# Weight splits and modulation sums behind evictions in the planner's order

## The chip, the cores and the metric

The kernel runs on one core of one Trainium2 chip. The time is device microseconds of one execution, as the median of several runs. Besides that there is one profiled execution, from which every duration below is read.

## What is computed

One token sequence (256 tokens, 1024 channels) passes through two networks in a row, all in float32. Cut to what matters:

```python
# first block (one layer)
h = rms_norm(x, g_mix_pre);  proj = h @ w_in                 # 1024 x 5376: q, k, v, pool, u, v, gates
merged = sum of three gated branches (stick-breaking attention, multiscale pool, spatial gating)
x = x + rms_norm(merged @ w_out, g_mix_post)
x = x + rms_norm(square(relu(rms_norm(x, g_ff_pre) @ w_ff_in)) @ w_ff_out, g_ff_post)
# second block, layer i = 0 (convolution), 1 (attention)
mod = silu(c) @ ada_w[i] + ada_b[i]                          # 1024 x 6144: sh1, sc1, g1, sh2, sc2, g2
h = rms_norm(x, mix_norm_g[i]) * (1 + sc1) + sh1
x = x + g1 * mixer(h)                                        # conformer_conv or moba_attention
h = rms_norm(x, mlp_norm_g[i]) * (1 + sc2) + sh2
x = x + g2 * (square(relu(h @ mlp_w1[i])) @ mlp_w2[i])
```

## The kernel before

All weights are streamed once from HBM, in one list called `stream`. An element of the list is 1 MB: either a `Half` (half of a weight block, 128 partitions x 2048 numbers) or an `Ada` (a quarter of one segment of the modulation weights). `issue_raw` (line 327) starts the load of the next elements into three `raw` buffers, by DMAs on the queue of SyncE (SP). `prep_one` (line 342) turns a landed element into what the engines use.

A `Half` is split into two float32r parts, since a float32 matmul is done as three float32r products: wH is the rounded copy (ScalarE, line 354) and wL the rest, raw minus wH (VectorE, line 355). Each is done in two parts of 128 x 1024, so a `Half` costs two ScalarE and two VectorE instructions. Four halves (two blocks) of wH and wL are held at a time (`W_SLOTS`). An `Ada` is not multiplied on TensorE at first: VectorE adds two products with the silu of c to an accumulator (line 383, two instructions of 128 x 1024). With the first quarter of a segment a bias row is loaded (line 377), and with some groups a GpSimd memset (line 370) and two gain rows (line 372). When a group is complete, `ada_finish` sums the accumulator over partitions by matmuls (line 395) and stores the rows, which `ada_load` brings back later.

`done` (line 431) is called when a block has been used: it frees its halves and calls `pump` (line 418), which prepares as many further elements as there are free slots. `need` does the same before a block is used. So the splits are traced, that is, written down by the program, between the work of one block and that of the next. Elements are prepared in two other places by `prep_one(by_part=True)`, for the first weights only.

What reads the results of TensorE are evictions: activations also are split into a high and a low part (`KM.split`, lines 508 and 509), the output of the stick-breaking attention is split by lines 820 and 821, gates are evicted by 851 and 852. The norms run over two token tiles: line 538 or 536 adds the parts of the sum, GpSimd raises it to the power -1/2 (line 539), VectorE scales, and TensorE transposes the result (line 514). `two_by_two` (line 893) is the stage with four jobs (two token tiles by two column blocks) and a norm after each token tile. `ff` (line 945) is the feed-forward, eight blocks in and eight blocks out. In the attention, line 1236 evicts the scores, lines 1238 to 1244 make the softmax and line 1253 transposes it.

The order of the instructions on each engine is not the order of tracing. A planner runs the traced program on a clock of its own: when an engine is free, it takes the instruction with the lowest number among those whose inputs are ready at that moment. The number is a counter, `tc.cur_priority`, that goes up by one with each traced instruction. On the chip each engine then works through its queue in exactly that order, whatever has become ready. In some stretches the order is the traced one by decree (`tc.manual_schedule`): all engines at the very start, and TensorE in the convolution stage.

Of the kernel before, what the change touches and what calls it, by code (L numbers as in the profile page):

```python
# [34 lines left out]
G0, G1 = (0, 1, 2, 3), (4, 5, 6, 7)  # L35
SB_AT = {(0, 0): (("s", G0),), (2, 1): (("c", G0),), (4, 1): (("o", G0), ("s", G1)), (6, 1): (("c", G1),), (8, 1): (("o", G1),)}
HOLD = 1
BASE_PAD = {"q4": 128, "hidH": 32, "ok": 144}
PUSH = {'pre': (0, 1, 0, 0, 0, 0), 'mix': (1, 2, 1, 2, 2, 1), 'ff': (1, 1, 1, 1, 1, 1, 1, 1, 1, 0, 1, 1, 1, 1, 1, 1), 'conv': (1, 4, 1), 'mlp': (1, 1, 1, 0, 1, 1, 1, 1, 1, 1, 1, 0, 1, 1, 0, 1), 'at': (0, 0, 0, 0)}

# [66 lines left out]
def net_kernel(ctx: ExitStack, tc: tile.TileContext, I, out):  # L107
# [8 lines left out]
    def nm(s):  # L116
        cnt[0] += 1
        return f"{s}_{cnt[0]}"
# [3 lines left out]
    def T(shape, tag, bufs, dt=F32):  # L122
        if tag in BASE_PAD and tag not in based:
            based.add(tag)
            sb.tile([P, BASE_PAD[tag]], F32, tag="pad" + tag, bufs=1, name=nm("pad"))
        return sb.tile(shape, dt, tag=tag, bufs=bufs, name=nm(tag))
# [7 lines left out]
    def dram(ap, offset, dims):  # L134
        return bass.AP(tensor=ap.tensor, offset=ap.offset + offset, ap=dims)
# [8 lines left out]
    stream = []  # L144
# [179 lines left out]
    st = {"raw": 0, "prep": 0, "gen": 0, "live": []}  # L324
# [15 lines left out]
    ada_ready = []  # L340

    def prep_one(by_part=False):
        i = st["prep"]
        it = stream[i]
        v = raws.pop(i)
        if isinstance(it, Half):
            kc, n = it.shape
            h = T([P, kc, n], "wH", W_SLOTS, F32R)
            l = T([P, kc, n], "wL", W_SLOTS, F32R)
            it.H, it.L = h, l  # L350
            st["live"].append(it)

            def part(p, q):
                act(h[:, p:q, :], v[:, p:q, :], AF.Copy)  # L354
                nc.vector.tensor_sub(l[:, p:q, :], v[:, p:q, :], h[:, p:q, :].bitcast(F32))  # L355

            m = kc // 2
            if by_part:
                st["prep"] += 1
                return [lambda: part(0, m), lambda: part(m, kc)]  # L360
            for p, q in ((0, m), (m, kc)):
                part(p, q)
        else:
            first = it.slot == 0 if len(it.group) == 1 else it.seg == it.group[0]
            if first and it.quarter == 0:
                acc_cur[0] = T([P, 2, D], "acc", 1)
                acc_cur[1] = T([P, 512], "adarow", 1)
                if 1 in it.group or 4 in it.group:
                    seg = 1 if 1 in it.group else 4
                    nc.gpsimd.memset(acc_cur[1], 1.0)  # L370
                    for n in range(2):
                        nc.sync.dma_start(acc_cur[1][32 * n:32 * n + 1, :],
                                          dram(I["mix_norm_g_2" if seg == 1 else "mlp_norm_g_2"],
                                               it.layer * D + n * 512, [[512, 1], [1, 512]]))
            acc = acc_cur[0][:, it.slot, :]
            if it.quarter == 0:
                nc.sync.dma_start(ada_init[0:1, :], dram(I["ada_b_2"], it.layer * 6 * D + it.seg * D, [[D, 1], [1, D]]))
                src = ada_init
            else:
                src = acc  # L380
            for c in range(2):
                k = it.quarter * 2 + c
                stt(acc, v[:, c, :], cond[:, k:k + 1], src, op0=ALU.mult, op1=ALU.add)  # L383
                src = acc
            if it.quarter == 3 and it.seg == it.group[-1]:
                ada_ready.append((it, acc_cur[0], acc_cur[1], st["gen"]))
        st["prep"] += 1
# [30 lines left out]
    def pump(limit=99):  # L418
        issue_raw()
        while st["prep"] < st["raw"] and limit > 0:  # L420
            it = stream[st["prep"]]
            if isinstance(it, Half):
                if len(st["live"]) >= W_SLOTS:
                    break
            elif ada_ready:
                break
            prep_one()
            issue_raw()
            limit -= 1

    def done(*blocks, limit=99):
        for b in blocks:
            for h in b.halves:
                st["live"].remove(h)
        ada_finish()
        st["gen"] += 1
        pump(limit)
# [154 lines left out]
    with tc.manual_schedule(engines={nc.tensor.engine, nc.vector.engine, nc.scalar.engine}):  # L592
# [17 lines left out]
        rst.append(norm_stats([x[1][:, half(n)] for n in range(2)]))  # L610
        hk.from_token_half(0, 0, h0[0])
        parts = prep_one(by_part=True)
        parts[0]()
        hk.from_token_half(0, 1, h0[1])
# [7 lines left out]
        v_part(1, 0)  # L622
        v_part(1, 1)
        parts = prep_one(by_part=True)
        for i in range(2):
            parts[i]()
# [646 lines left out]
    def flush(keep=0):  # L1273
        while len(pend) > keep:
            qk_trans(*pend.pop(0))

    for n in range(2):
        bq, bk = B["aq", n], B["ak", n]
        need(bq, bk)
        for t in range(NT):  # L1280
            for i, b in enumerate((bq, bk)):
                a = ts_job(hk, t, b)
                qn = qk_norm(a)
                if t == 1:
                    done(b)
                flush(HOLD)
                pend.append((n, t, i, qn))
# [85 lines left out]
```

## Time and profile before

| | |
|---|---|
| median of 3 runs | 994.72 us (992.79 to 997.69) |
| profiled execution, whole | 991.49 us |
| its span, first to last instruction | 989.8 us |
| busy TensorE, weight loads of it | 962.0 us, 790.5 us |
| busy VectorE, ScalarE, GpSimd | 709.7, 544.8, 63.4 us |
| wL subtractions (line 355) | 306, 1.22 us each |
| wH copies (line 354) | 306, 1.05 us each |
| modulation sums (line 383) | 84 and 12, 1.28 us each |
| read from HBM | 221.44 MB, 225 GB/s over the span |

In the timelines a row is the start in us from the span's start, the duration, the engine, the line, the operation, output and inputs by the program's names, the shapes, and how many like instructions follow each other in it. A bracket is the idle time of the engine before it and what ended it. PE is TensorE, DVE is VectorE, ACT ScalarE, POOL GpSimd, SP SyncE.

### The profile page before, as it was taken

What the parts mean: (1) busy time and instruction counts of PE and PEld (TensorE: products, weight loads), DVE (VectorE), ACT (ScalarE), POOL (GpSimd) and SP (SyncE); (2) the same over time, 40 slices, a digit from 0 to 9 for tenths busy, and PEclk for the clock granted to TensorE, in tenths of its full rate; (3) what the DMA queues carried; (4) which work ended last, traced back from release to release, by engine and by line L of the source; (5) the groups of instructions that cost most, each with busy time, mean ns of one, the idle gap of its engine ahead of it and who ended that gap; (6) DMA issues with size and microseconds to landing.
All of it is one profiled execution on the core that took longest, in us unless ns stands there. A gap on an engine that the chain in (4) does not pass through costs nothing.

```text
span 989.8 us, 12826 instructions
## 1 busy us (share of the span) xinstructions
PE 962.0 (97%) x4969; PEld 790.5 (80%) x4969; DVE 709.7 (72%) x914; ACT 544.8 (55%) x835; POOL 63.4 (6%) x88
## 2 busy tenths in 40 slices
PE   7999999999999999998999999999989999999998
PEld 5988879878788887864878888887867778888886
DVE  6758877788677777888678677768678486665553
ACT  5646765456655565423555665555576456555561
POOL 4102110010000000100000000001330000000000
PEclk9999999999999999999999999999999999999999
DMA  7788676578678986785258888875524246676531
GB/s 253 246 297 278 225 280 209 196 253 287 210 270 294 313 309 206 242 302 192 76 173 299 287 286 284 309 255 197 189 86 170 86 165 218 218 249 246 200 130 43
DMA packets 89731, 223.37 MB, mean 226 GB/s; under 512 B 4304, under 2 KB 8298, under 8 KB 89670
## 3 DMA queue, kind: packets, MB, share of 16 engines
q1 hardware_dynamic: 89670, 222.55, 65.0%
q8 instruction: 39, 0.64, 0.3%
q14 instruction: 22, 0.18, 0.0%
HBM read 221.44 MB, written 1.10 MB: 225 GB/s over the span
## 4 chain that ended last, share of the span: by engine, by line
PE 74%; DVE 13%; issue 4%; ACT 3%; DMA 3%; POOL 2%; POOLq 0%; SPq 0%; DVEq 0%; ACTq 0%
PE B L469 14%; PE A L456 13%; PE A L454 13%; PE A L455 13%; PE B L470 7%; DVE wL L355 5%; PE A L469 3%; DMA raw<-in_w_in_dram 2%; DVE acc L383 2%; ACT wH L354 2%; POOL rst L539 1%; PE A L461 1%; PE A L463 1%; PE A L462 1%; PE A L470 1%
## 5 line engine op out<-in xcount | busy, mean ns | idle before, releaser
L355 DVE TENSOR_TENSOR wL<-raw,wH 128x1024 fp32r<-128x1024 f32 x306 | 362.0, 1221 | 109.8 <-ACT wH L354 109.4
L354 ACT ACTIVATE wH<-raw 128x1024 fp32r<-128x1024 f32 x306 | 306.9, 1051 | 176.4 <-PE A L456 99.4
L469 PE MATMUL B<-hHL,wH 128*128 128x512 f32 x576 | 204.1, 399 | 0.0
L470 PE MATMUL B<-hHL,wL 128*128 128x256 f32 x576 | 162.0, 281 | 0.0
L454 PE MATMUL A<-wH,hidH 128*128 128x512 f32 x384 | 151.2, 394 | 0.0
L456 PE MATMUL A<-wH,hidL 128*128 128x512 f32 x384 | 150.0, 391 | 0.0
L455 PE MATMUL A<-wL,hidH 128*128 128x512 f32 x384 | 149.8, 390 | 0.0
L454 PE MATMUL A<-wH,hHL 128*128 128x512 f32 (+1 forms) x336 | 130.9, 390 | 1.5 <-ACT wH L354 0.8
L469 PEld LDWEIGHTS B<-hHL,wH 128*128 128x128 f32 x576 | 108.3, 188 | 27.4 <-ACT wH L354 0.8
L455 PE MATMUL A<-wL,hHL 128*128 128x512 f32 (+1 forms) x336 | 129.5, 385 | 0.5 <-DVE wL L355 0.5
L456 PE MATMUL A<-wH,hHL 128*128 128x512 f32 (+1 forms) x336 | 129.5, 386 | 0.0
L383 DVE SCALAR_TENSOR_TENSOR acc<-raw,cond,acc 128x1024 f32<-128x1024 f32 x84 | 107.9, 1285 | 17.2 <-DMA raw<-in_ada_w_dram 16.7
L470 PEld LDWEIGHTS B<-hHL,wL 128*128 128x128 f32 x576 | 109.0, 189 | 0.7
L454 PEld LDWEIGHTS A<-wH,hidH 128*128 128x128 f32 x384 | 72.1, 188 | 18.0 <-issue 3.3
L456 PEld LDWEIGHTS A<-wH,hidL 128*128 128x128 f32 x384 | 72.1, 188 | 15.5
L455 PEld LDWEIGHTS A<-wL,hidH 128*128 128x128 f32 x384 | 72.2, 188 | 14.3
L454 PEld LDWEIGHTS A<-wH,hHL 128*128 128x128 f32 x336 | 63.7, 190 | 15.0 <-issue 1.6
L455 PEld LDWEIGHTS A<-wL,hHL 128*128 128x128 f32 x336 | 63.7, 190 | 12.9 <-DVE wL L355 1.0
L456 PEld LDWEIGHTS A<-wH,hHL 128*128 128x128 f32 x336 | 63.8, 190 | 12.6 <-issue 0.3
L469 PE MATMUL A<-hHL,wH 128*128 128x512 f32 x192 | 68.2, 400 | 2.1 <-DVE hidL L821 2.1
L470 PE MATMUL A<-hHL,wL 128*128 128x256 f32 x192 | 53.7, 280 | 0.0
L976 ACT ACTIVATE rs<-B 128x256 f32<-128x256 f32 x72 | 27.1, 376 | 48.2 <-PE B L470 48.2
(238 smaller groups left out, 1177.8 us busy)
## 6 DMA issues: line engine op xcount, KB each, us to landing
raw<-in_mlp_w_dram SPq DMA_DIRECT2D x64, 1024.0 KB
raw<-in_ada_w_dram SPq DMA_DIRECT2D x48, 1024.0 KB
raw<-in_w_in_dram SPq DMA_DIRECT2D x19, 1024.0 KB
raw<-in_w_ff_in_dram SPq DMA_DIRECT2D x16, 1024.0 KB
raw<-in_w_ff_out_dram SPq DMA_DIRECT2D x16, 1024.0 KB
raw<-in_attn_w_qkv_dram SPq DMA_DIRECT2D x12, 1024.0 KB
raw<-in_conv_w_in_dram SPq DMA_DIRECT2D x8, 1024.0 KB
ada<-mod SPq DMA_DIRECT2D x24, 256.0 KB
```

The source lines that it names most:

```text
L354: act(h[:, p:q, :], v[:, p:q, :], AF.Copy)
L355: nc.vector.tensor_sub(l[:, p:q, :], v[:, p:q, :], h[:, p:q, :].bitcast(F32))
L383: stt(acc, v[:, c, :], cond[:, k:k + 1], src, op0=ALU.mult, op1=ALU.add)
L454: mm(dst, lh(xc), wh, start=s0, stop=False)
L455: mm(dst, lh(xc), wl, start=False, stop=False)
L456: mm(dst, ll(xc), wh, start=False, stop=s1)
L461: mm(dst, wh, rh(xc), start=(i == 0), stop=False)
L462: mm(dst, wh, rl(xc), start=False, stop=False)
L463: mm(dst, wl, rh(xc), start=False, stop=(i == len(kcs) - 1))
L469: mm(dst, wh, km.HL[:, :, k, :], start=(k == 0), stop=False)
L470: mm(dst[:, 0:S], wl, km.HL[:, 0, k, :], start=False, stop=(k == KC - 1))
L976: act(r1[:, s, :], a[:, S:2 * S], AF.Copy)
```

## The change

`prep_one` becomes a wrapper. It raises the planner's counter by 60 for a weight half and by 120 for a modulation quarter, traces the same preparation as before, and takes the same amount off again. All that the preparation issues is traced under the raised counter: the splits or the accumulations, and with an `Ada` also its bias row, memset and gain rows. The raw loads are issued outside of it and keep their numbers. The preparation by part at the start is left as it was.

```diff
+LAG = {True: 60, False: 120}
@@
     def prep_one(by_part=False):
+        if by_part:
+            return prep_at(by_part)
+        p = tc.cur_priority
+        lag = LAG[isinstance(stream[st["prep"]], Half)]
+        tc.cur_priority = p + lag
+        prep_at(False)
+        tc.cur_priority -= lag
+
+    def prep_at(by_part):
         i = st["prep"]
         it = stream[i]
         v = raws.pop(i)
```

## Rows read from the trace of the kernel before

**Rows 1.** The page: busy us, share of the span, instructions

```profile
PE 962.0 (97%) x4969; PEld 790.5 (80%) x4969; DVE 709.7 (72%) x914; ACT 544.8 (55%) x835; POOL 63.4 (6%) x88
```

**Rows 2.** Table of stretches: length, busy us (instructions) by engine, clock, DMA

```profile
215.00:380.00 165.00, 165.00 (x820) 135.78 (x818) 123.58 (x132) 93.85 (x136) 0.53 (x1) 1.00 0.79 275
```

**Rows 3.** TensorE's waits: tile, line <- releaser: us in total, times, longest

```profile
PE B L514 <- DVE rs L565: 4.0, 5, 1.2
PE B L1253 <- DVE w L1243: 3.1, 2, 1.8
...
PE A L469 <- DVE hidL L821: 2.1, 1, 2.1
...
PE B L514 <- DVE rs L563: 1.7, 2, 0.9
PE A L454 <- ACT q L508: 1.6, 1, 1.6
PE B L1107 <- DVE hidL L1101: 1.5, 1, 1.5
PE B L731 <- DVE rs L701: 1.4, 1, 1.4
```

**Rows 4.** Line 355: duration min/median/max in ns; TensorE's waits for it

```profile
L355 DVE TENSOR_TENSOR wL<-raw,wH x306: 1207/1219/1320, 11.1 to 966.8; 128x1024 fp32r<-128x1024 f32 x153
...
  PE A L455: 0.5, 1
```

**Rows 5.** Timelines, 136 to 141 us: ScalarE, VectorE, TensorE

```profile
136.15 0.64 ACT L820 ACTIVATE hidH<-A 128x256 fp32r<-128x256 f32 x2
...
138.79 1.28 DVE L383 SCALAR_TENSOR_TENSOR acc<-raw,cond,acc 128x1024 f32<-128x1024 f32 x1
139.99 0.42 DVE L821 TENSOR_TENSOR hidL<-A,hidH 128x256 fp32r<-128x256 f32 x1
...
140.46 0.50 PE L469 MATMUL A<-hHL,wH 128*128 128x512 f32 x1 [2.13 <-DVE hidL L821]
```

**Rows 6.** Timelines, 40 to 51 us: ScalarE, VectorE, TensorE

```profile
40.49 0.19 ACT L699 ACTIVATION_READ_ACCUMULATOR junk<-rs 128x1 f32 x1
...
42.03 1.28 DVE L383 SCALAR_TENSOR_TENSOR acc<-raw,cond,acc 128x1024 f32<-128x1024 f32 x1
43.22 0.21 DVE L538 TENSOR_SCALAR rst<-ss 128x1 f32<-128x1 f32 x2
...
49.09 1.23 DVE L355 TENSOR_TENSOR wL<-raw,wH 128x1024 fp32r<-128x1024 f32 x1 [2.80 <-ACT wH L354]
...
50.86 0.40 PE L731 MATMUL B<-ada,rs 128*64 128x128 f32 x2 [1.44 <-DVE rs L701]
```

**Rows 7.** Timelines, 733 to 748 us: VectorE, TensorE

```profile
733.56 2.35 DVE L355 TENSOR_TENSOR wL<-raw,wH 128x1024 fp32r<-128x1024 f32 x2
...
743.00 3.49 DVE L355 TENSOR_TENSOR wL<-raw,wH 128x1024 fp32r<-128x1024 f32 x3
...
747.01 0.55 PE L1253 MATMUL B<-ident,w 128*128 128x128 f32 x3 [0.48 <-DVE w L1236]
```

**Rows 8.** Timelines, 794 to 811 us: GpSimd, VectorE, TensorE

```profile
794.59 0.55 POOL L539 TENSOR_TENSOR rst<-rst,neghalf 128x1 f32<-128x1 f32 x1 [53.14 <-DVE rst L536]
808.40 1.47 POOL L539 TENSOR_TENSOR rst<-rst,neghalf 128x1 f32<-128x1 f32 x1 [13.26 <-DVE rst L536]
...
808.23 1.22 DVE L355 TENSOR_TENSOR wL<-raw,wH 128x1024 fp32r<-128x1024 f32 x1
...
810.71 0.66 PE L514 MATMUL B<-ident,rs 128*128 128x128 f32 x4 [0.84 <-DVE rs L565]
```

**Rows 9.** Timelines, 811 to 815 us: VectorE, TensorE

```profile
811.23 1.22 DVE L355 TENSOR_TENSOR wL<-raw,wH 128x1024 fp32r<-128x1024 f32 x1
...
814.85 0.39 PE L455 MATMUL A<-wL,hHL 128*128 128x512 f32 x1
```

**Rows 10.** Waits of SyncE's queue, longest in total

```profile
SPq L334 <- DVE wL L355: 559.9, 120, 22.0
```

## What I expect, and why

> **What bounds the kernel now.** I read the busy shares of the page first. TensorE is busy 962.0 of the span's 989.8 us, VectorE 72%, ScalarE 55% [rows 1]. The table of stretches then says where TensorE is the limit outright: in 215 to 380 it is busy for all 165.00 us, and the two other feed-forward stretches (525 to 670, 825 to 975) read the same, busy from end to end [rows 2]. In these 460 us nothing that VectorE or ScalarE does sooner can shorten the run. What can be won is the idle time of TensorE elsewhere, 989.8 - 962.0 = 27.8 us, and part of that is the first load and the tail after the last matmul. So the third view is the list of what TensorE waited for. The waits that stand at places where the planner is free to reorder sum to 4.0 + 3.1 + 2.1 + 1.7 + 1.4 = 12.3 us, and two more, 1.6 + 1.5 us, belong to the convolution stage [rows 3]. That is the whole field: about 15 us, 1.5%.
>
> The fourth view is who waits for the splits themselves. A split costs 1.22 us on VectorE, there are 306 of them, and TensorE waited once, 0.5 us, for the result of one [rows 4]. The weights are ahead of their use, so there is room to push them back. That is what the change relies on.
>
> **The change, part by part.** It adds and removes no instruction. The planner, which writes each engine's queue before the run, gives a free engine the ready instruction with the lowest number, and the number is the order of tracing. The change adds 60 to weight splits (one wH copy on ScalarE and one wL subtraction on VectorE per part) and 120 to the modulation accumulations. So an instruction changes place only where a split or an accumulation was traced before an eviction or a norm step, by less than the lag, and both were ready. A split that only fills a gap, because nothing else is ready, stays. The numbers below are therefore a hunt for places of the first kind ahead of which TensorE waits.
>
> (A) 136 to 140 us, the eviction of the attention output (line 821). ScalarE has its half of both evictions done at 136.79, yet the first VectorE half starts at 139.99, behind accumulations of 1.28 us, the last at 138.79, and splits that were traced earlier; it releases a bank, and TensorE waits 2.13 us for it [rows 5]. Two of the instructions ahead of it are gone by the new numbers, and one in progress may remain. I take 2.1 us; bounds 0 (the planner's own clock has the eviction ready later) and 2.13.
>
> (B) 40 to 51 us, the norm of the gating branch. Its sum is ready at 40.68, its next step (line 538) starts at 43.22, behind a split and an accumulation; its last step (line 701) then stands behind a split at 49.09 that had itself waited 2.80 us, and the matmul at its end waits 1.44 us [rows 6]. Begun about 2.4 us sooner, the last step is ready well before that split and should be planned ahead of it. I take 1.4; bounds 0 and 1.44.
>
> (C) 733 to 747 us, attention scores. The score evictions (line 1236) stand behind 2.35 us of splits at 733.56 and again behind 3.49 us at 743.00; TensorE waits 0.48 us at 747.01, and twice, 3.1 us in all, for line 1243, which follows them [rows 3, 7]. Only the shorter of these two (3.1 - 1.8 = 1.3 us) lies behind the splits. I take 1.2; bounds 0 and 0.48 + 1.3 = 1.8.
>
> (D) The ends of the norms, seven waits of the transposes (line 514), 4.0 + 1.7 us [rows 3]. Here the splits were traced after the norm and have the higher number already. They sit under the GpSimd power instead: it takes 0.55 us alone and 1.47 us while a wL subtraction runs beside it (808.23 and 808.40), 0.92 us more, and the transposes behind it wait 0.84 us [rows 8]. A lag doesn't empty that gap, since nothing else is ready in it. I take 0; bounds -5.7 us (all gone) and, if deferred splits fill gaps that are free today, a loss of 0.92 for each.
>
> The Trainium skill speaks against a gain here. SBUF — State Buffer, section Who interferes with whom, says in effect that a VectorE instruction with two SBUF inputs and a GpSimd instruction that reads SBUF exclude each other, and the later one blocks until the first is done. The trace agrees: 0.55 against 1.47 us [rows 8]. By that rule pushing splits back from evictions gains nothing wherever they land under a power, and my (D) of 0 would be a small minus.
>
> (E) The convolution stage, 1.6 + 1.5 us [rows 3]: TensorE's order is written by hand, and the accumulations there fill gaps. I take 0, bounds plus and minus 3.1.
>
> (F) What else moves with a prepared tile. The accumulation branch also issues twelve bias rows and eight gain rows on SP (lines 372 and 377) and four GpSimd memsets (line 370), which now rank behind raw weight loads. SP's raw loads already wait 559.9 us for wL subtractions to free a raw buffer [rows 10]; a bias row queued behind one waits too. The cover is that no wait of TensorE for an accumulation is in the list at all [rows 3]. A later split also frees its raw buffer later, by the same 1 to 3 us; the cover is the distance to the first use. At zero, then; if that cover goes, a price as in the slower rival below.
>
> Sum: 2.1 + 1.4 + 1.2 = 4.7 us. The profiled execution took 991.49 us (its span 989.8 and 1.7 around it), so it would take 986.8. It lies 3.2 below the median of the runs, 994.72; taken off that median, 994.7 - 4.7 = 990.0 us. The bounds of (A) to (C) alone give gains of 0 to 5.4 (2.13 + 1.44 + 1.8).
>
> **The rivals.** *Nothing reaches TensorE.* The planner also places TensorE's instructions by its own clock; if the chain comes earlier there, the transposes are placed earlier too and wait as long. For it: the waits are short (under 2.2 us) as small differences between plan and chip would be. Against it: (A) is a bank release, not a place in an order. Time 994.7, between 993 and 996. Chance 0.17.
>
> *The powers are freed.* If the new order puts an eviction instead of a split in those gaps, or has the splits done before, then (D) pays as well: 4.7 + 5.7 = 10.4 us, 984.3 (982 to 987). For it: eight powers are stretched today like the one at 808.40 [rows 8]. Against it: the splits are pushed towards these gaps, not away. The skill's rule cited under (D) belongs to this rival: with the splits out of the gaps it would give this time. Chance 0.15.
>
> *Late weights, slower.* The place is the entry of a stage, where the eight splits of two blocks share VectorE with the norm of the second token tile. The last of them ends at 811.23 + 1.22 = 812.45, and the matmul that reads it is at 814.85: 2.40 us, two splits' worth [rows 9]. From that point on a deferral turns into a wait of TensorE. If the last pair slips by four splits (4.9 us) at each of the five entries (near 215, 405, 505, 690, 813), it costs 5 x (4.9 - 2.4) = 12.5 us, less the 4.7 gained: 7.8 slower, 1002.5; with three splits' slip (3.7 us) it is 6.5 lost, 996.5. For it: a lag of 60 is nearly a block's 64 matmuls. Against it: the splits still fill every gap, and the norm before them is over at 811.3. Chance 0.18.
>
> *The change does nothing* (numbers not obeyed, same queues) is counted with the first rival.
>
> **How the numbers follow.** Forecast 0.50: gains of 2 to 8 us, 987 to 993, the excess over 5.4 being places with no TensorE wait of their own that shift others; just over half of it, 0.26, lies past 5 us. A measurement of this kernel can tell about 0.5%, 5 us, from no change. Faster: 0.26 + 0.15 = 0.41. Within: 0.24 + 0.17 = 0.41. Slower 0.18. The range takes in the freed powers' middle and the lower part of the late weights, 983.5 to 1000.5, and leaves out about 0.06 below and 0.1 above. The likeliest case's own range is 987 to 993.
>
> **What would show it.** (A) right: no wait of line 469 for hidL line 821, and line 821 directly behind line 820's end. (B) right: line 538 near 41 us and no wait of line 731. (C) right: line 1236 ahead of line 355 near 733 and 743. (D) right: the powers of second-tile norms still at 1.4 to 1.5 us and the transposes still waiting 0.8. The nothing rival: the same sum of TensorE's waits, at moved places. Freed powers: all near 0.55. Late weights: waits of lines 454 and 455 for wH and wL, which today make one of 0.5 us, at stage entries. The prediction is wrong if TensorE's busy time itself changes, or if accumulations appear among its releasers.

## The result, and the profile after

| | before | after |
|---|---|---|
| median of the runs made together | 993.28 us (5 runs) | 986.99 us (986.63 to 989.09) |
| the same once more, on another chip | 992.98 us (9 runs) | 985.16 us (984.72 to 987.23) |
| profiled execution, its span | 991.49, 989.8 us | 986.63, 984.9 us |

The ratio of the medians is 0.9939, with a 95% interval of 0.9918 to 0.996, and the second time 0.993 (0.9917 to 0.9944). The change is worth some 6 to 8 us. The time lies inside the range on record and 3.0 us under the predicted 990.0. In the lines below the lines of the code are 10 higher than before from line 343 on, and one higher ahead of it: 365 is the wL subtraction (355 before), 393 the modulation sum (383), 464 to 466 the weight matmuls (454 to 456).

The page of the changed kernel, beside [rows 1], and below it that of the second profile (after_again, span 983.3 us):

```profile
PE 961.7 (98%) x4969; PEld 790.5 (80%) x4969; DVE 709.1 (72%) x914; ACT 545.3 (55%) x835; POOL 61.0 (6%) x88
...
PE 959.7 (98%) x4969; PEld 789.4 (80%) x4969; DVE 709.4 (72%) x914; ACT 545.0 (55%) x835; POOL 61.9 (6%) x88
```

In the first profile TensorE is busy about as long as before, but only because its clock was lower for 6.8 us near 250, which made its matmuls longer there (below). In the second profile the clock fell where it fell before the change, near 470 and 724. There TensorE is busy 2.3 us less than before, 959.7 against 962.0, and the other 4.2 us of the shorter span are idle time. So not only waits went: the planner has also changed the order of TensorE's own matmuls, near 36 to 52, 200, 730 to 763 and 777 us.

TensorE's waits of the changed kernel (tile, line <- releaser: us in total, times, longest), beside [rows 3]:

```profile
PE B L524 <- DVE rs L575: 4.0, 5, 1.2
...
PE B L1263 <- DVE w L1253: 1.8, 1, 1.8
PE A L464 <- ACT q L518: 1.6, 1, 1.6
PE B L1117 <- DVE hidL L1111: 1.5, 1, 1.5
PE B L524 <- DVE rs L573: 1.5, 2, 0.8
...
PE B L1242 <- DVE w L1246: 0.6, 1, 0.6
PE A L465 <- DVE wL L365: 0.5, 1, 0.5
```

The rows of line 469 (479 now) for line 821 and of line 731 (741) for line 701 are gone, of the two for line 1243 (1253) the shorter one is gone. Two short waits of line 1242 (1232) are new in the attention, 0.60 us for a score eviction and 0.35 for ScalarE. The norm ends (524) and the convolution (464 for q, 1117) stand as they did. The last row answers [rows 4]: one wait for a wL, 0.5 us, as before.

Where TensorE gained and lost is read by matching each matmul of the two programs by its tiles and comparing the starts. The differences, medians over stretches of the kernel before, in us (negative is earlier):

```
before, us:    37-42  54-100  145-195  225-246  270-380  478-490  700-715  800-980
after           0.44   -2.34    -4.73    -4.88    -1.66    -2.95    -2.98    -4.86
after_again     0.38   -2.41    -4.79    -4.83    -4.83    -4.51    -4.55    -6.47
```

Three steps down are the same in both executions: 2.8 us near 50, 2.4 us near 138, 1.9 us between 715 and 800. A step up of 3.2 us near 250, and 1.3 us back near 470, belong to the first execution alone; they are the granted clock (below).

*Near 138* (timelines of ScalarE and VectorE; beside [rows 5]):

```profile
133.01 0.39 ACT L830 ACTIVATE hidH<-A 128x256 fp32r<-128x256 f32 x1 [0.29 <-PE A L828]
133.72 0.75 DVE L831 TENSOR_TENSOR hidL<-A,hidH 128x256 fp32r<-128x256 f32 x2
134.38 1.27 DVE L393 SCALAR_TENSOR_TENSOR acc<-raw,cond,ini 128x1024 f32<-128x1024 f32 x1
```

The VectorE halves of the two evictions follow ScalarE's at 133.72 and the sum comes behind them; before it was the other way round, and the eviction 3.2 us behind ScalarE.

*Near 50* (timelines of VectorE and TensorE, beside [rows 6]; then the table of stretches, from the same matmul to the same matmul, before and after):

```profile
39.82 0.15 DVE L548 TENSOR_SCALAR rst<-ss 128x1 f32<-128x1 f32 x1
...
41.92 0.15 DVE L548 TENSOR_SCALAR rst<-ss 128x1 f32<-128x1 f32 x1
...
43.53 0.88 DVE L711 SCALAR_TENSOR_TENSOR rs<-rs,rst,ada 128x256 f32<-128x256 f32 x2
...
45.20 1.09 PE L741 MATMUL B<-ada,rs 128*64 128x128 f32 x16
...
51.34 1.28 DVE L393 SCALAR_TENSOR_TENSOR acc<-raw,cond,ini 128x1024 f32<-128x1024 f32 x1
```

```profile
36.00:53.00 17.00, 15.56 (x136) 14.44 (x135) 11.26 (x15) 9.83 (x15) 3.77 (x3) 1.00 0.80 246
```

```profile
36.00:50.66 14.66, 14.66 (x136) 14.18 (x135) 9.99 (x14) 10.25 (x17) 2.27 (x3) 1.00 0.73 235
```

The two sums that stood at 39.70 and 42.03 now begin at 51.34, the norm's last step has moved from 50.24 to 43.53, and the matmul behind it waits for nothing. For the same 136 matmuls TensorE had 1.44 us of idle time and 15.56 us busy; now it has none and 14.66. The 0.90 us of busy time are not simply the wait's, for the order differs: the sixteen matmuls of line 741 (731) now follow in one row, behind others of their kind, and before a matmul of line 463 stood between the second and the third of them (TensorE's timeline of before):

```profile
51.19 0.38 PE L463 MATMUL A<-hHL,wL 128*128 128x256 f32 x1
51.51 1.09 PE L731 MATMUL B<-ada,rs 128*64 128x128 f32 x14
```

How much of the 0.90 us is the order's and how much the wait's, no run separates.

*Attention scores* (VectorE and TensorE, beside [rows 7]):

```profile
727.45 0.55 DVE L1246 SCALAR_TENSOR_TENSOR w<-cst,B 128x384 f32<-128x384 f32 x1 [0.52 <-PE B L1242]
...
738.71 1.01 DVE L1246 SCALAR_TENSOR_TENSOR w<-cst,B 128x384 f32<-128x384 f32 x2
...
740.68 1.22 DVE L365 TENSOR_TENSOR wL<-raw,wH 128x1024 fp32r<-128x1024 f32 x1
...
742.92 0.49 PE L1242 MATMUL B<-q,q 64*128 64x128 f32 x2 [0.35 <-ACT q L1229]
```

The first score eviction has an early place of its own, the later ones stand ahead of the splits, and what TensorE waits for next is 0.35 us, for ScalarE. In this stage TensorE's waits sum to 3.75 us before and 2.75 after, so about 1.0 us of the step of 1.9 is theirs. The rest has no wait in it: the matmuls of lines 1303 and 1304 (1313 and 1314), which multiply the softmax with v, stood mingled in ones to threes near 777 and now stand in fours. The table of stretches for the same 34 matmuls, 32 of them of these lines, before and after, with one row of TensorE's timeline from each:

```profile
777.57 0.32 PE L1304 MATMUL A<-q,gb 128*64 128x128 f32 x1
776.49:780.33 3.84, 3.83 (x34) 2.69 (x33) 3.13 (x4) 2.88 (x6) 0.00 (x0) 1.00 0.87 285
```

```profile
773.17 0.40 PE L1314 MATMUL A<-q,gb 128*64 128x128 f32 x4
772.69:775.49 2.80, 2.80 (x34) 2.37 (x33) 2.35 (x3) 2.71 (x5) 0.00 (x0) 1.00 0.81 236
```

*The powers and the entry* (GpSimd, VectorE, TensorE, beside [rows 8, 9]; then SyncE's longest wait, beside [rows 10]):

```profile
385.47 0.55 POOL L549 TENSOR_TENSOR rst<-rst,neghalf 128x1 f32<-128x1 f32 x1 [2.92 <-DVE rst L546]
386.95 1.29 PE L524 MATMUL B<-ident,rs 128*128 128x128 f32 x8 [1.19 <-DVE rs L575]
...
803.55 1.46 POOL L549 TENSOR_TENSOR rst<-rst,neghalf 128x1 f32<-128x1 f32 x1 [13.27 <-DVE rst L546]
803.39 1.21 DVE L365 TENSOR_TENSOR wL<-raw,wH 128x1024 fp32r<-128x1024 f32 x1
805.85 0.66 PE L524 MATMUL B<-ident,rs 128*128 128x128 f32 x4 [0.84 <-DVE rs L575]
806.38 1.22 DVE L365 TENSOR_TENSOR wL<-raw,wH 128x1024 fp32r<-128x1024 f32 x1
809.99 0.39 PE L465 MATMUL A<-wL,hHL 128*128 128x512 f32 x1
```

```profile
SPq L335 <- DVE wL L365: 494.1, 111, 20.4
```

Near 804 nothing has changed but the moment: the split under the power, 1.46 us, the wait of 0.84, the last split 2.4 us ahead of its first use. Note the first two rows: the longest wait of this kind stands behind a power that nothing stretches.

*The clock* (table of stretches of the first profile of the changed kernel; the third number from the end is the granted clock). Of the two levels, 2.4 and 1.2 GHz, the lower one was granted for 6.8 us, from about 252, at the end of the eight matmuls of the tap table over 31 rows (line 931); a 512-column matmul then took 0.63 us instead of 0.39 (a row of TensorE's timeline during the fall; at 809.99 above it is 0.39).

```profile
246.00:264.00 18.00, 18.00 (x62) 12.47 (x61) 8.97 (x10) 8.02 (x13) 0.00 (x0) 0.81 0.58 197
```

```profile
253.35 0.63 PE L465 MATMUL A<-wL,hidH 128*128 128x512 f32 x1
```

### The profile page after: what moved, and what is told of

The parts are those of the page before. It is cut to its first block, busy times and chain, and to the rows that moved or that the text cites. A ratio compares the mean times of both kernels' runs of the same rounds, so it can differ in the third digit from the quotient of the medians.

```text
span 984.9 us, 12815 instructions
## 1 busy us (share of the span) xinstructions
PE 961.7 (98%) x4969; PEld 790.5 (80%) x4969; DVE 709.1 (72%) x914; ACT 545.3 (55%) x835; POOL 61.0 (6%) x88
## 4 chain that ended last, share of the span: by engine, by line
PE 82%; DVE 10%; issue 2%; POOL 2%; ACT 2%; DMA 1%; POOLq 0%; SPq 0%; ACTq 0%
PE A L466 14%; PE A L464 14%; PE A L465 14%; PE B L479 14%; PE B L480 7%; PE A L479 5%; DVE wL L365 4%; PE A L480 2%; PE A L471 2%; PE A L472 2%; PE A L473 2%; POOL rst L549 1%; PE A L1095 1%; PE B L524 1%; DVE rs L568 1%
```

## The experiments

All kernels but before_taps_128 are edits of the changed kernel. Each was timed in rounds with the kernel before (medians of 993.0 to 993.3 us). The table gives the TensorE starts against the kernel before at the same stretches as above; the column 37-42 is mostly the start of the run and not the change (see the last section), so the steps between columns are what to read.

```
before, us:           37-42  54-100  145-195  225-246  270-380  420-440  700-715  800-980
halves_only           -0.03    0.42    -0.71     0.10     0.10     4.63     3.08     1.21
sums_only              1.93   -0.86    -3.24    -3.02    -3.02    -3.02    -3.00    -3.06
early_only             2.13   -0.66    -3.04    -3.14    -1.51    -1.50    -3.17    -3.16
late_only              0.18    0.56    -0.16    -0.24    -0.24    -0.24     0.03    -1.82
lags_swapped           1.02   -1.77    -2.51    -2.32     0.56     5.04     1.92     0.22
taps_128               0.37   -2.41    -4.80    -4.83    -5.19    -5.20    -6.48    -8.32
lag_x16_taps_128       0.96   -1.82    -4.05    -3.95    -4.32    -4.32    -5.60    -7.48
sums_only_taps_128     0.25   -2.53    -4.92    -4.70    -5.03    -5.03    -5.06    -5.04
```

### Which lag does what

```diff
-LAG = {True: 60, False: 120}
+LAG = {True: 60, False: 0}      # halves_only
+LAG = {True: 0, False: 120}     # sums_only
```

> Only the weight halves get the lag of 60, the modulation sums keep their old number. Theory (each gained wait had both kinds ahead of it): at 136 to 140 us a sum of 1.28 us still stands right ahead of the eviction of line 821 in the order of before, so about 0.8 us of its 2.13 us wait comes back at most; at 40 us a sum again delays line 548 (538 before), so that the 1.44 us wait of line 741 comes back; the attention gain of 1.9 us stays, since there are only splits there. About 3 us less than before in all: 990. Rival (the splits alone do it): the same as the changed kernel, 987, with both early waits gone. Either way the clock of 250 to 258 us is looked at: if the loss of 3.2 us there hangs on the moment at which that stretch is reached, it can be absent here.

> Only the modulation sums get the lag of 120. Theory: the 1.44 us wait of line 741 at 50 us goes (the sum ahead of line 548 goes away), with up to 0.9 us more as in the changed kernel; at 138 us some of the 2.13 us wait goes; in the attention, where no sums run ahead of line 1246, nothing is gained, and its waits stay at 3.1 us. About 2 to 3 us less than before: 991. Rival (the splits alone do it): no gain, 993.3.

With the halves alone the median was 993.08 us, ratio 0.9996 (0.9984 to 1.0009): no gain at all. With the sums alone it was 988.43, ratio 0.9947 (0.9935 to 0.9959), most of the whole. Both expectations were wrong in part. The steps say why. The gain near 50 is 2.79 us with the sums alone and absent with the halves alone. The gain near 138 is 2.4 us with the sums alone; with the halves alone it is there as well (1.68 to -0.71 between 116 and 140), but a new wait near 116 eats 1.1 of it, for an eviction (line 862) that stands behind a split and, further ahead, a sum. The attention's 1.9 us is the halves' alone. And with the halves alone 4.5 us are lost near 405. TensorE's waits in this kernel, then VectorE's timeline there and the table of the stretch that follows (the third number from the end is the granted clock):

```profile
PE A L465 <- DVE wL L365: 3.4, 4, 2.6
...
PE B L741 <- DVE rs L711: 1.9, 1, 1.9
...
PE A L479 <- DVE ada L862: 1.1, 1, 1.1
```

```profile
401.69 1.27 DVE L393 SCALAR_TENSOR_TENSOR acc<-raw,cond,acc 128x1024 f32<-128x1024 f32 x1
...
404.74 1.28 DVE L393 SCALAR_TENSOR_TENSOR acc<-raw,cond,acc 128x1024 f32<-128x1024 f32 x1
405.93 1.28 DVE L519 TENSOR_TENSOR hHL<-B,hHL 128x512 fp32r<-128x512 f32 x2
407.13 2.35 DVE L365 TENSOR_TENSOR wL<-raw,wH 128x1024 fp32r<-128x1024 f32 x2
```

```profile
408.00:412.00 4.00, 3.60 (x9) 2.86 (x10) 1.48 (x2) 0.00 (x0) 0.00 (x0) 0.57 0.93 316
```

VectorE in the changed kernel, the same norm:

```profile
399.89 1.21 DVE L365 TENSOR_TENSOR wL<-raw,wH 128x1024 fp32r<-128x1024 f32 x1
...
402.88 1.22 DVE L365 TENSOR_TENSOR wL<-raw,wH 128x1024 fp32r<-128x1024 f32 x1
404.02 1.28 DVE L519 TENSOR_TENSOR hHL<-B,hHL 128x512 fp32r<-128x512 f32 x2
405.22 1.27 DVE L393 SCALAR_TENSOR_TENSOR acc<-raw,cond,acc 128x1024 f32<-128x1024 f32 x1
```

There are two gaps, one behind each step of the norm of the second tile. Two splits fill them in the changed kernel and two sums with the halves alone; then the splits come after the eviction of line 519, and TensorE waits 2.6 us for a wL. Behind that wait the granted clock is 0.57 for four microseconds, which makes up the rest of the 4.5. This is the prediction's slower rival, at one of its five entries.

### Which of the two comes first

```diff
+LAG = {True: 120, False: 60}    # lags_swapped
```

> The two lags exchanged: 120 for the weight halves, 60 for the modulation sums, so that both are still behind evictions and norms but a sum now stands ahead of a half. With only the halves lagged, TensorE waited 2.6 us at the entry of a stage (405 us) for a wL, since the sums took the gaps under the two powers and the split came after line 519. Theory (what decides is which of the two fills these gaps): the same wait of 2 to 3 us at 405 us and perhaps at other entries, the early gains (A) and (B) and (C) kept; 989 to 991 us. Rival (the size of the lag on the halves costs nothing as long as the sums are lagged too): the same as the changed kernel, 987.

991.41 us, ratio 0.9977 (0.9959 to 0.9995). The gains near 50 and in the attention are there. That near 138 is there too, but new waits and a changed order between 104 and 140 eat most of it (0.7 us is left by the table). And 4.5 us are lost near 405, as with the halves alone:

```profile
PE A L465 <- DVE wL L365: 3.0, 2, 2.6
```

So it isn't being put back that makes weights late, but being put behind something that takes their gap. That the sums' lag is the larger one is what keeps the gain.

### Where in the kernel

```diff
         lag = LAG[isinstance(stream[st["prep"]], Half)]
+        if st["prep"] >= stream.index(B["out", 0].halves[0]):   # late_only: <
+            lag = 0
```

> Both lags, but only for what is prepared ahead of the output projection (up to about 195 us); from there on the numbers are those of before. Theory: the two early gains stay whole, so that TensorE is 4.7 us ahead of before at 200 us, and the attention gain of 1.9 us is lost. If the loss of 3.2 us at 250 us is brought by the moment alone, it is here as well, and the result is about 1.5 to 2.8 us under before (990.5 to 992); if it is brought by the later order of the splits, it is not here, and the result is 4.7 us under before (988.5).

> Both lags, but only from the output projection on; all before it is as in the kernel before. Theory: nothing is gained up to 200 us, 1.9 us in the attention (line 1263's waits for line 1253 from 3.1 us to 1.8), so about 991.4. If the clock loss at 250 us is brought by the later order of the splits, it is here too and the result is 994.6, slower than before; if by the moment at which TensorE gets there, the granted clock stays 1.00 from 250 to 258 us.

Early only: 988.77 us, ratio 0.9951 (0.9935 to 0.9967). Late only: 991.53, ratio 0.9989 (0.9976 to 1.0002). The early kernel has the steps of 2.79 and 2.38 us and nothing in the attention, the late one the attention's 1.85 and nothing near 50 (a 0.7 us step near 138 is there too, although nothing is changed there: that wait was 1.4 us long in this execution, 2.1 in the profile of before). The three places are independent of each other. The early kernel has the order of before from 195 us on, and the clock fell near 250 all the same: the later splits are not its cause; and in the late kernel, which has them, it did not fall there. The early kernel's single runs spread from 986.2 to 991.5 us, so its median says little on the fall.

### The clock fall near 250

```diff
         dw = T([P, D], "q4", 4)
+        nc.gpsimd.memset(dw, 0.0)
@@
-                mm(pt, cv["tab"][:TAPS, TF + j * P:TF + (j + 1) * P], dw[:TAPS, n * 512:(n + 1) * 512],
+                mm(pt, cv["tab"][:, TF + j * P:TF + (j + 1) * P], dw[:, n * 512:(n + 1) * 512],
```

> The changed kernel with the eight convolution-weight matmuls of line 931 over 128 rows in place of 31 (the tap tile is zeroed first, and the rows past 31 of the table are zeros, so the result is the same). Same order on TensorE. In the changed kernel the granted clock falls to 0.50 during these matmuls and stays there for some 6 us; in the kernel before and in three of four kernels so far it didn't, with the same matmuls. Theory: the few rows are what the fall hangs on; with 128 rows the clock stays 1.00 from 246 to 264 us and the 3.2 us come back, 983.8 us. Rival: the rows have nothing to do with it, and the fall comes or not by the moment: the clock of that stretch is 0.81 again and the time 987; or the zeroing delays the tap tile and a new wait of a few us stands ahead of line 931.

> The control: the same 128-row matmuls in the kernel before, whose clock is 1.00 from 246 to 264 us. Theory: nothing changes there, 993 us, and the eight matmuls take 3.70 us as with 31 rows. Rival: the rows are worth something beyond the clock fall, and this kernel is faster as well.

> The changed kernel once more, unchanged, for one question: is the clock fall at 250 us a property of its order or of one execution? It showed in the profile of the changed kernel (clock 0.81 over 246 to 264 us) and in three of the six other kernels with 31-row taps, one of which has the order of the kernel before from 195 us on. Theory (it comes or not by the moment, and the first matmuls wait for a DMA that lands up to 1.5 us sooner or later from one execution to the next): this time the fall can be absent or of another length, and the times of the single runs spread over the same 3 us, 984 to 990, median 987. Rival (a property of the order): again 0.81 there, with the fall from about 251 to 258 us, and a median of 987.

The changed kernel with 128-row taps took 984.42 us, ratio 0.99 (0.9873 to 0.9926), with lag_x16_taps_128 below (984.40) the lowest of the versions that compute all; the kernel before with them 992.74, ratio 0.9981 (0.9962 to 1.0). The changed kernel itself, profiled a second time, had no fall. The stretch in that second profile, and with 128-row taps:

```profile
246.00:264.00 18.00, 18.00 (x77) 13.28 (x76) 9.85 (x11) 9.89 (x15) 0.00 (x0) 1.00 0.57 196
```

```profile
246.00:264.00 18.00, 18.00 (x79) 13.67 (x78) 10.20 (x12) 10.25 (x16) 0.00 (x0) 1.00 0.55 201
```

So the fall is a matter of the single execution and no property of the new order; the rival of the third text above is out. Whether the 128 rows prevent it stays open. Of nine profiles with 31 rows (with no_pow below) four show it; of five with 128 rows none does. That points to the rows, but the intervals of the times, 0.9873 to 0.9926 against 0.9917 to 0.9944, still overlap. The mean granted clock of the single runs points the same way: 0.994 to 0.997 in the ten runs of the changed kernel, 0.996 to 0.998 in the 18 runs of the three kernels with 128 rows and both lags. But it doesn't say where in a run the clock fell.

### How far back is too far

```diff
+LAG = {True: 960, False: 1920}
```

> Both lags sixteen times as large (960 and 1920, past a whole stage's instructions), on the kernel with 128-row taps, to keep the clock fall out of it. The slower rival of the prediction: deferral by more is deferral that reaches TensorE. Theory (the splits and sums still fill every gap in which nothing else is ready, so the lag saturates: after the planner VectorE's queue differs from that of the smaller lags in a few places between 60 and 190 us and hardly later): 984.4 us as with 60 and 120, within 1 us, no new wait of lines 464 and 465. Rival (late weights): waits of 2 us and more for wH or wL at the entries of the stages, 990 us or more.

> Only the modulation sums lagged, on the kernel with 128-row taps: what the lag of the weight halves is worth by itself. Theory: the gains (A) and (B) are the sums' alone, the halves bring the attention's 1.9 us and nothing else; 986.3 us, with 3.1 to 3.3 us of waits of line 1264 for 1254 instead of 1.8. Rival (the halves bring nothing that can be measured): 984.4 us as with both.

984.4 us and ratio 0.9921 (0.9904 to 0.9938) with sixteen times the lag, against 984.42 with the small one: no difference, and no wait for a wL beyond 0.5 us. The lag saturates. The sums alone: 987.18, ratio 0.9942 (0.9929 to 0.9955), with the longer attention wait, so that the halves' lag is worth 2.8 us by the medians, 1.9 by the starts.

```profile
PE B L1264 <- DVE w L1254: 3.3, 2, 1.8
```

### What the norm ends wait for

```diff
-        nc.gpsimd.tensor_tensor(rs, rs, neg_half, op=ALU.pow)
+        vts(rs, rs, 0.0, 1.0, op0=ALU.mult, op1=ALU.add)      # no_pow
```

```diff
-                nc.vector.tensor_sub(l[:, p:q, :], v[:, p:q, :], h[:, p:q, :].bitcast(F32))
+                for s in (slice(0, n // 2), slice(n // 2, n)):   # wl_in_two_taps_128
+                    nc.vector.tensor_sub(l[:, p:q, s], v[:, p:q, s], h[:, p:q, s].bitcast(F32))
```

> The changed kernel, in which the norms leave out the power -1/2 (VectorE writes ones in its place, in a small instruction of some 0.2 us; the norms then don't normalise, all else is computed). It bounds what the waits of the transposes (line 524) behind the norms hang on. Theory: they hang on GpSimd's power, 0.55 us alone and 1.47 us beside a split; without it most of the 5.5 us of line 524's waits for lines 575 and 573 is gone, 982 us. Rival: the split that fills the gap under the power holds VectorE itself; without the power the planner still puts a split there or the next one is as late, and less than 2 us is gained, 985 us or more.

> Each wL subtraction of 128 x 1024 in two instructions of 128 x 512, on the kernel with 128-row taps. The powers that are stretched from 0.55 to 1.40 to 1.47 us then share VectorE with an instruction half as long. Theory (the power waits until the subtraction beside it is over): the stretched powers take about 0.55 + 0.4 = 1.0 us or less, and the five waits of line 524 that lie behind them shrink by 0.4 us each; 2 us less, 982.5 us. Rival: the second half follows at once and holds the power as before, or the fixed cost of 306 more instructions (about 0.1 us each on VectorE) delays the splits at the entries: 984.4 us or more.

Without the powers: 977.45 us, ratio 0.9826 (0.9789 to 0.9863), and the waits of line 524 behind the norms fall from 5.5 to 0.2 us. Its data are other data, and its three timed runs had a granted clock of 1.000 where the other kernels had 0.991 to 0.998, so not all of the 9 us is the power's; its profiled execution, with 0.996, is 5.9 us shorter than that of the changed kernel. Nor is its vanished wait the power's length alone: at six norms its transposes stand 5 to 11 matmuls later in TensorE's queue (near 803 they begin with the 4113th matmul, with the power with the 4107th). With the subtractions in two: 986.68 us, ratio 0.9936 (0.9924 to 0.9948), 2.3 us slower than with 128-row taps alone; most of that is the attention, where TensorE's waits sum to 5.3 us and not to 2.8. Here a step of the argument broke. Timelines of GpSimd and TensorE in that kernel (its lines are one to two higher), at the same norm as above, then its wait in all:

```profile
802.82 0.93 POOL L550 TENSOR_TENSOR rst<-rst,neghalf 128x1 f32<-128x1 f32 x1 [12.47 <-DVE rst L547]
...
804.59 0.66 PE L525 MATMUL B<-ident,rs 128*128 128x128 f32 x4 [0.84 <-DVE rs L576]
```

```profile
PE B L525 <- DVE rs L576: 4.2, 5, 1.2
```

The power is shorter by half a microsecond, 0.93 instead of 1.46, as expected, and the wait behind it is 0.84 us exactly as before. The order of TensorE is different: with the shorter subtractions the transposes of six norms stand one to six matmuls earlier in its queue (at this norm they begin with the 4101st and no longer with the 4107th). The likely reading is that the planner also sees a shorter chain and moves the transposes up by as much, so that the wait is the part of the chain that the planner doesn't count. The planner's own clock is in no trace, so this reading is not shown; the row behind the unstretched power at 385.47, 1.19 us, fits it. The rule of the Trainium skill named in the prediction (SBUF — State Buffer, section Who interferes with whom) holds: the power was blocked no longer than the instruction beside it lasts, now 0.68 us. Near 43 us in the kernel before it was held longer, through two subtractions in a row (last section). But the block isn't what these waits are made of.

## Why the prediction was right or wrong

The direction was right, and so was the mechanism for the waits of (A), (B) and half of (C): an eviction or a norm step that was ready stood behind a sum or a split, and now stands ahead of it. The forecast case was gains of 2 to 8 us; the measured one is 6.3 and 7.8, and the median, 986.99, lies on the edge of that case's own 987 to 993. What the sum had no term for is that the planner rearranges TensorE's own queue too. That is worth up to some 2 us (busy time 962.0 before, 959.7 in the second profile), and the prediction named a change of TensorE's busy time as a sign of being wrong; here its account was incomplete.

- (A), taken as 2.1, is 2.4 us in both profiles, and 2.2 to 2.4 in every kernel that has a sums' lag of 120 or more in this stretch. TensorE's order is unchanged here, so the wait cost 0.3 us more than its 2.13: the first matmul behind it took 0.50 us, those that follow 0.40. In two other profiles with the old order (late_only, before_taps_128) this wait was 1.4 and 1.5 us and that of (B) 1.8 in place of 1.44, so the split between the two terms is uncertain by 0.7 us.
- (B), taken as 1.4 with 1.44 as the upper bound, is 2.3 us at the end (2.8 from 37 to 54, of which 0.4 is four transposes done earlier). This is a term that was mis-sized, and its bound was wrong in kind: only the wait was counted, but the matmuls around it, in their old order, were also busy 0.90 us longer, 15.56 against 14.66 us. One of the two powers on this path took 2.65 us before, beside two subtractions in a row, and takes 0.55 now; the prediction's rows did not have it.
- (C), taken as 1.2 with a bound of 1.8, is 1.7 to 1.9 us in each of the seven profiles in the tables that have the halves' lag there and whole subtractions. That it comes close to the bound is luck. Of the two waits behind line 1243 only the shorter went, as foreseen, and the 0.48 us for line 1236 too; but 0.60 and 0.35 us are new, so that the waits gave about 1.0 us. The other 1.0 is the order of lines 1303 and 1304 near 777, a place that the prediction did not list.
- (D), taken as nothing, is nothing: 4.0 + 1.5 us after, 4.0 + 1.7 before. The reason given for the zero held: eight powers are stretched after the change as before it. What failed is the price behind its bounds, that a power freed of the split would take its wait away: a shorter power doesn't shorten the wait (wl_in_two_taps_128). What fits is the first half of the rival "nothing reaches TensorE": the planner places the transposes by its own clock.
- (E) and (F), taken as nothing: the waits of 1.6 and 1.5 us stand, and no wait for a bias row or a sum appeared. SP's wait for wL became shorter, 494.1 us [rows 10 had 559.9], that for the sums longer, 106.3 us against 72.3. Lines 454 and 455 had not one wait for a split before, as the prediction says, but two: 0.8 us for a wH copy stands in the list of before and after alike.
- The sum of the terms by the starts is 2.3 + 2.4 + 1.9 + 0.1 = 6.7 us against 4.7. In the first profile the clock took 3.2 back near 250 and gave 1.3 near 470. By the medians 1.6 us of the miss of 3.0 are the larger gain, 6.3 against 4.7, and 1.4 the median of before: 994.72 on three runs, 993.28 on the five beside the result and 993.0 to 993.3 on all the sets of 5 to 23.
- Late weights: the mechanism is real and its price was too low for one entry and too high for five. It came at one entry only and cost 4.5 us there, a wait of 2.6 and the clock behind it, where the prediction had 2.5 for each. Its condition was named wrongly: not how far the halves are pushed back (sixteen times the lag costs nothing), but whether a sum is allowed into their gap. "The splits still fill every gap" was right only because the sums rank behind them.
- Powers freed: out, as (D) shows. That the change does nothing is out as well.

## What to carry to other kernels

Putting preparation work behind evictions in a planner's order pays where an eviction is ready and stands behind it, and it costs nothing while the pushed work still finds the gaps that nothing else fills. Where two kinds of work are pushed back, the one without a due time must rank last, since they compete for the same gaps: here that decided between 6 us gained and 0 to 2. A planner that orders all engines also changes the queue of the busiest one: compare its order before putting a gain down to a wait. And a wait that stays when the work ahead of it becomes shorter may be one that the planner doesn't count; see whether the waiting instruction has moved up in its queue.

## What the runs showed of the hardware

- The granted clock fell, to 0.50 in the first profile of the changed kernel, behind eight fp32 matmuls over 31 rows in four of nine profiled executions, the same program among both kinds, and cost 3.2 us where it was longest (6.8 us). In the convolution stage (448 to 476) it was 0.94 in half of the profiles and 1.00 in the others, worth 1.2 to 1.6 us. In the attention, near 724, it fell for 3.4 us in ten of the fourteen at no cost: in sums_only it didn't, and TensorE gained nothing on the kernel before (-3.00 and -3.06 us in the table), since its waits there sum to 4.5 us in place of 3.75. A difference of 2 to 3 us between single executions of this kernel can be that alone.
- The DMA of a small table (w_spatial) let TensorE wait 0, 0.7 or 1.5 us near 36 us, with the same order of TensorE there:

```profile
PE B L694 <- DMA ada<-in_w_spatial_dram: 1.5, 1, 1.5
```

That row is of early_only; in the changed kernel there is none. With the start of the run (up to 0.9 us) and four transposes that stand earlier in the new order (0.4 us) it makes the column 37-42 of the tables.
- A wait of TensorE of 2.13 us cost 2.4 us where the order of its matmuls stayed the same (near 138).
- GpSimd's power took 0.55 us alone, 0.93 beside one subtraction of 0.68 us, 1.46 beside one of 1.22, and 2.65 where two of 1.22 followed each other (43.45 in the kernel before): it was held through both.
- The order of unlike matmuls has a price of its own: the same 34 matmuls, 32 of them of 256 and 128 columns, took 3.84 us mingled and 2.80 us in rows of four (near 777).
